# One mixer moved to the head of both transformer layers, and the attention steps moved off its products

## The chip, the cores and the metric

The kernel runs on one core of one Trainium2 chip. The metric is the device time of one execution in microseconds (us). The core has five engines that run beside each other: TensorE (PE, with its weight loads shown apart as PEld), VectorE (DVE), ScalarE (ACT), GpSimd (POOL) and SyncE (SP, which issues most DMAs). In the trace each engine's instructions stand in the order of its own list; where an operand isn't there yet the engine stands still, and what is behind in its list with it.

## The reference, cut to what matters

A first block (a Hyena layer, then grouped attention) is followed by a second block of two layers. The change lies in these two, so only they matter here. `x` has 256 tokens, and in the first of the two layers 256 context tokens go through the same work.

```
def trunk_layer(...):
    h = modulate(rmsnorm(x, g1), sh1, sc1)
    z = h @ w_in
    ...
    o = diff_attend(q, k, v, lam)                       # 4 heads, two score maps each
    mix = concat([mixer_a(z), mixer_b(z), mixer_c(z), diff_out(o)])
    x = x + gt1 * (mix @ w_out)
    x = x + gt2 * conv_ffn(...)

def mixer_a(z, ws, bs):
    u = gelu(group(z, G_AU))
    v = rmsnorm(gelu(group(z, G_AV)))                   # per head
    mixed = einsum('hpq,bcqhd->bcphd', ws, v) + bs
    return u * mixed
def mixer_b(z, w):  return group(z, G_BB) * dwconv3(group(z, G_BC) * group(z, G_BX), w)
def mixer_c(z):     return real(fft2(group(z, G_CF)))
```

The three mixers and the attention read only `z`; their shares of `mix @ w_out` are summed, so they may be computed in any order.

## The kernel before

Features lie on the partitions, tokens on the columns: n = 512 columns in layer 0 of the last block (256 latent and 256 context tokens) and n = 256 in layer 1. Every product is made in three passes over a high and a low half of each operand (`mm3`, lines L285 to L287: hi by hi, lo by hi, hi by lo). Weights come as 512 KB pieces (`wr`), which ACT casts to the high half `wh` (L281) and DVE subtracts for the low half `wl` (L282). A projection of a mixer (`proj_f`) is 24 such passes into one PSUM tile of the tag `mm`; there are four of these tiles, handed out in turn, so a tile comes back when its fourth predecessor has been read.

In each of the two layers this comes first: keys (`keys`, `heads_t(1)`), and then queries (`queries`, `heads_t(0)`), the latter two tokens blocks t = 0 and 1. `queries` turns q by a table on DVE (L1149 to L1156), splits and transposes it (`stack`, L1126, L1127, L1130, L1137), and also makes `gv` for mixer a out of the same PSUM tile: a gelu on ACT (L1167), a square and a sum on DVE (L1170, L1171, L374), a power on POOL (L378), and a scaling on DVE (L1174). In layer 0 the attention of the context tokens (`attend(range(4))`) is run to its end between keys and queries.

The attention of the latent tokens (`last4`) is a generator of 10 steps. A step holds for one q block the scores and two exponentials (`maps`, L1207 to L1214), for one two steps back its transposes (`turn`, L1224), and on every other one the product with v (`values`, L1233). After them stands the norm of the attention's result (`norm_d`, two parts). The steps are taken from a list `turns` of 13 entries, `[last4] * 10 + [nd, None, nd]`, one at each call of `turn_of`, and these calls stand behind the products of the mixers and, in `out_x`, behind every so many of the 8 output products (`every`). So a mixer or an output product is a carrier under whose PE work a step of attention runs.

`ORDER` sets which mixer comes first. In layer 0 the first mixer's output product follows it at once with a turn after each second product; in both layers the output product of mixer i comes behind mixer i + 1. Mixer a (`mixer_a`) multiplies `gv` by a table on PE (L1287, tile `pa`) between a gelu of its projection (L1282) and two DVE passes (L1290, L1292). Mixer c makes two small products one behind the other, with a split on ACT and DVE between.

The text of the kernel is not the order on the engines: a scheduler lists each engine's instructions by what it takes to be ready, and the loads of ACT's function tables (ACT_TABLE_LOAD, wherever the next function isn't in the table that is loaded) are put in behind it.

Of the kernel before, what the change touches and what calls it, by code (L numbers as in the profile page):

```python
# [32 lines left out]
STEPS = (2, 1, 2, 1)  # L33

LAG_G, LAG_D = (1, 3), (2, 2)
ORDER = ("bac", "cab")

N_ADA = 96
PACE = 0.6
# [193 lines left out]
def build(nc, tc, a, out, off, upto=99):  # L233
    with ExitStack() as es:
        _build(es, nc, tc, a, out, off, upto)


def _build(es, nc, tc, a, out, off, upto):
# [13 lines left out]
    def mmps(n=512):  # L252
        return pmm.tile([P, 512], F32, tag="mm", name="mm")[:, :n]
# [16 lines left out]
    def tmb(n=512):  # L270
        return rg.tile([P, 512], F32, tag="tb", bufs=4, name="tb")[:, :n]
# [4 lines left out]
    def pair(pool, shape, tag, bufs=1):  # L276
        return _Pair(pool.tile(shape, F32R, tag=tag + "h", name=tag + "h", bufs=bufs),
                     pool.tile(shape, F32R, tag=tag + "l", name=tag + "l", bufs=bufs))

    def split(dst, src):  # L280
        S.copy(dst.hi, src)  # L281
        V.tensor_tensor(dst.lo, src, dst.hi.bitcast(F32), op=ALU.subtract)  # L282
# [6 lines left out]
    def load_w(src, pool=None, step=True):  # L289

        raw = wp.tile([P, 1024], F32, tag="wr", bufs=NWR, name="wr")
        nc.sync.dma_start(raw, src.rearrange("p k c -> p (k c)"))
        if step:
            ada_step()
            av_step()
        w = pair(pool or wp, list(src.shape), "w", NW)
        split(w, raw.rearrange("p (k c) -> p k c", k=src.shape[1]))
        return w

    def load_c(src, i, step=True):  # L300

        return [load_w(src[2 * i + j], step=step) for j in range(2)]

    def proj_f(ps, w, h, cols, kt=8, m=0):
        for k in range(kt):
            mm3(ps, w[:, k, m * P:(m + 1) * P], h[:, k, cols], k == 0, k == kt - 1)
# [139 lines left out]
    def proj_o(ps, prods, m, c):  # L446

        for i, (ws, act) in enumerate(prods):
            for k in range(2):
                mm3(ps, ws[m // 4][:, k, (m % 4) * P:(m % 4 + 1) * P], act[:, k, c],  # L450
                    i + k == 0, i == len(prods) - 1 and k == 1)
# [3 lines left out]
    def turn_of():  # L455

        if turns:
            f = turns.pop(0)
            if f:
                next(f, None)  # L460

    def out_x(prods, n, gts, every=0):

        for m in range(8):
            ps = mmps(n)
            proj_o(ps, prods, m, slice(0, n))
            add_x(ps, m, n, gts)
            if every and m % every == every - 1:
                turn_of()
# [30 lines left out]
    def add_x(ps, m, n, gts):  # L500
        for j in range(n // 256):
            c = slice(256 * j, 256 * j + 256)
            V.scalar_tensor_tensor(xt[:, m, c], ps[:, c], gts[j][:, m:m + 1], xt[:, m, c],  # L503
                                   op0=ALU.mult, op1=ALU.add)
# [78 lines left out]
    def ada_upto(l, q):  # L583

        ada_step(max(0, 8 * (ada_q0[l] + q) - ada_done[0]))
        if ada_done[0] <= 8 * (ada_q0[l] + q) or ada_done[0] == N_ADA:
            ada_flush()
# [32 lines left out]
    def mod_part(l, v, part):  # L620
        return ada[l][:, v, 8 * part:8 * part + 8]
# [458 lines left out]
    for l in range(2):  # L1080
        ctx_out = l == 0
        n = 512 if ctx_out else 256
# [21 lines left out]
        gt1 = [mod_part(al, v, 2) for v in range(2)]  # L1104

        def mixer_w(j):

            if l == 0:
                ada_upto(al, 3)
            return [load_w(a["w_o"][l, c, j]) for c in range(2)]  # L1110
# [161 lines left out]
        def mixer_a(tag):  # L1272
            gws = tmb().rearrange("p (h s) -> p h s", h=4)
            nc.sync.dma_start(gws, a["gws"][l])
            w = load_c(a["w_f"][l], 0)
            mix = pair(a3, [P, 2, n], tag, 1 if tag == "at" else 512 // n)
            for m in range(2):
                ps = mmps(n)
                proj_f(ps, w[m], h, slice(0, n))
                turn_of()  # L1280
                gu = tmb(n)
                S.activation(gu, ps, AF.Gelu_apprx_tanh)  # L1282
                pa = mmps(n)
                for t in range(nt):
                    for hh in range(2):
                        hd = 2 * m + hh
                        T.matmul(pa[64 * hh:64 * hh + 64, t * P:t * P + P], gv[:, t, 64 * hd:64 * hd + 64], gws[:, hd, :],  # L1287
                                 start=True, stop=True, tile_position=(0, 64 * hh))
                ga = tmb(n)
                V.tensor_tensor(ga.rearrange("p (t q) -> p t q", q=P), pa.rearrange("p (t q) -> p t q", q=P),  # L1290
                                gbs[:, l, m, :].unsqueeze(1).to_broadcast([P, nt, P]), op=ALU.add)
                V.tensor_tensor(ga, ga, gu, op=ALU.mult)  # L1292
                split(mix[:, m, :n], ga)
            return mix
# [58 lines left out]
        held = None  # L1353
        for i, c in enumerate(ORDER[l]):
            mix = {"a": mixer_a, "b": mixer_b, "c": mixer_c}[c]("at" if i == 2 else "mix")
            if held:
                out_x([(mixer_w("abc".index(held[0])), held[1])], n, gt1, 4)
            held = c, mix
            if i == 0 and l == 0:
                out_x([(mixer_w("abc".index(c)), mix)], n, gt1, 2)  # L1360
                held = None
        while turns:
            turn_of()
        if l == 0:
            ada_upto(al, 5)
        ws = [[load_w(a["w_o"][l, c, j]) for j in ("abcd".index(ORDER[l][-1]), 3)] for c in range(2)]
        prods = [([ws[0][i], ws[1][i]], m) for i, m in enumerate((mix, mixd))]
# [89 lines left out]
```

## Time and profile before

| | |
|---|---|
| median of 3 runs | 1809.03 us (1806.14 to 1810.25) |
| the profiled execution | 1808.75 us, its span 1807.0 us |
| PE busy in the span | 1757.9 us (97%) |
| DVE busy, ACT busy | 1354.5 us (75%), 814.6 us (45%) |
| granted clock of TensorE, mean | 0.991 |
| layer 0's mixers and attention | 966 to 1060 us of the span |
| layer 1's mixers and attention | 1519 to 1600 us of the span |

PE's busy time is that of overlapping passes; a pass of 512 columns starts 0.23 us behind the last one when nothing is waited for, one of 256 columns 0.117 us. Where PE's next start is later than that, PE has stood still, and since it is busy nearly throughout, such time is what a change of order can add or remove.

### The profile page before, as it was taken

How to read it: one execution, taken by the hardware profiler on the slowest of the kernel's cores; microseconds unless marked ns; L12 is line 12 of the kernel's file. 1: busy time of each engine (PE TensorE's matmuls, PEld its weight loads, DVE VectorE, ACT ScalarE, POOL GpSimd, SP SyncE). 2: the span in 40 equal slices, each digit the busy share in tenths (PEclk: the TensorE clock that was granted, in tenths of full speed). 3: DMA queues.
4: the chain of work that ended last, by engine and by line, in shares of the span. 5: the costliest groups of instructions: out<-in, count | busy, mean ns of one | idle time of the engine just before them, and what ended most of it. 6: DMA issues, size and time to landing. Idle time of an engine off the chain costs nothing.

```text
span 1807.0 us, 27447 instructions
## 1 busy us (share of the span) xinstructions
PE 1757.9 (97%) x10602; PEld 1480.7 (82%) x10602; DVE 1354.5 (75%) x2449; ACT 814.6 (45%) x1447; POOL 43.0 (2%) x42
## 2 busy tenths in 40 slices
PE   6999999999999999999999999999999999999998
PEld 2778788787777888888878889788888887989997
DVE  6778577577666776888968867988667777878786
ACT  3433233334233354556578526332332337654444
POOL 0000000000000001000000000000000000000000
PEclk8999999999999999999999999999999999999999
DMA  8454434444444433333443223544544553346662
GB/s 333 173 175 161 147 130 139 152 147 137 140 155 146 151 111 118 118 113 119 144 141 115 76 68 101 180 147 154 157 151 145 194 175 112 106 129 199 187 186 83
DMA packets 73889, 262.62 MB, mean 145 GB/s; under 512 B 8288, under 2 KB 9632, under 8 KB 73120
## 3 DMA queue, kind: packets, MB, share of 16 engines
q1 hardware_dynamic: 71328, 254.71, 43.4%
q10 hardware_dynamic: 1856, 3.28, 0.6%
q0 software_dynamic: 576, 2.88, 0.5%
q8 instruction: 84, 1.38, 0.3%
q14 instruction: 45, 0.37, 0.1%
HBM read 259.79 MB, written 1.05 MB: 144 GB/s over the span
## 4 chain that ended last, share of the span: by engine, by line
PE 88%; DVE 6%; ACT 2%; issue 1%; DMA 1%; POOL 1%; SPq 0%; POOLq 0%; DVEq 0%; ACTq 0%
PE mm L285 25%; PE mm L286 24%; PE mm L287 24%; PE at L285 3%; PE at L287 2%; PE at L286 2%; PE ad L541 2%; DVE wl L282 1%; POOL rs_r L378 1%; PE tp L1011 1%; ACT wh L281 1%; PE tp L1130 1%; PE tp L1224 1%; PE at L388 1%; DVE t L412 1%
## 5 line engine op out<-in xcount | busy, mean ns | idle before, releaser
L281 ACT CAST wh<-wr 128x1024 fp32r<-128x1024 f32 x328 | 342.7, 1050 | 555.1 <-PE mm L286 493.4
L285 PE MATMUL mm<-hh,wh 128*128 128x512 f32 (+1 forms) x1568 | 550.0, 352 | 2.3 <-ACT hh L427 1.1
L286 PE MATMUL mm<-hl,wh 128*128 128x512 f32 (+1 forms) x1568 | 545.1, 348 | 1.1 <-DVE hl L844 1.1
L287 PE MATMUL mm<-hh,wl 128*128 128x512 f32 (+1 forms) x1568 | 544.0, 348 | 0.5 <-DVE wl L282 0.5
L282 DVE TENSOR_TENSOR wl<-wr,wh 128x1024 fp32r<-128x1024 f32 x328 | 399.2, 1219 | 189.0 <-ACT wh L281 188.3
L285 PEld LDWEIGHTS mm<-hh,wh 128*128 128x128 f32 x1568 | 295.0, 189 | 56.5 <-issue 11.9
L287 PEld LDWEIGHTS mm<-hh,wl 128*128 128x128 f32 x1568 | 295.0, 188 | 40.1 <-DVE wl L282 0.9
L286 PEld LDWEIGHTS mm<-hl,wh 128*128 128x128 f32 x1568 | 295.4, 189 | 38.5 <-DVE hl L844 1.7
L503 DVE SCALAR_TENSOR_TENSOR xt<-mm,ada,xt 128x256 f32<-128x256 f32 x352 | 153.6, 477 | 26.6 <-PE mm L287 25.2
L285 PE MATMUL mm<-fh,wh 128*128 128x256 f32 (+1 forms) x384 | 124.7, 326 | 0.4 <-DVE xt L503 0.4
L286 PE MATMUL mm<-fl,wh 128*128 128x256 f32 (+1 forms) x384 | 124.7, 326 | 0.0
L287 PE MATMUL mm<-fh,wl 128*128 128x256 f32 (+1 forms) x384 | 124.6, 325 | 0.0
L602 DVE CUSTOM_DVE_ANT_0 junk<-av,cb,vec 128x1024 f32<-128x1024 f32 x64 | 82.0, 1281 | 28.4 <-DMA av<-in_ada_dram 27.8
L285 PE MATMUL mm<-wh,hh 128*128 128x512 f32 x240 | 96.6, 405 | 3.1 <-DVE t L920 2.3
L286 PE MATMUL mm<-wl,hh 128*128 128x512 f32 x240 | 96.0, 400 | 0.7 <-DVE wl L282 0.7
L287 PE MATMUL mm<-wh,hl 128*128 128x512 f32 x240 | 96.1, 401 | 0.0
L378 POOL TENSOR_TENSOR rs_r<-rs_x,mhalf 128x4 f32<-128x4 f32 (+2 forms) x34 | 40.4, 1191 | 1719.7 <-DVE rs_x L374 1583.4
L285 PEld LDWEIGHTS mm<-fh,wh 128*128 128x128 f32 x384 | 72.7, 190 | 7.4 <-DVE xt L503 0.6
L286 PEld LDWEIGHTS mm<-fl,wh 128*128 128x128 f32 x384 | 72.9, 190 | 6.7
L287 PEld LDWEIGHTS mm<-fh,wl 128*128 128x128 f32 x384 | 72.8, 190 | 6.6
L541 PE MATMUL ad<-ar,sc_c 128*32 128x256 f32 x768 | 56.9, 407 | 5.7 <-DMA ar<-in_ada_dram 5.7
L286 PE MATMUL mm<-al,wh 128*128 128x512 f32 (+1 forms) x160 | 56.4, 354 | 0.0
(347 smaller groups left out, 2932.5 us busy)
## 6 DMA issues: line engine op xcount, KB each, us to landing
ar<-in_ada_dram SPq DMA_DIRECT2D x96, 512.0 KB, 4.4
wr<-in_w_u_dram SPq DMA_DIRECT2D x88, 512.0 KB, 3.7
wr<-in_hy_in_dram SPq DMA_DIRECT2D x64, 512.0 KB, 4.6
av<-in_ada_dram SPq DMA_DIRECT2D x48, 512.0 KB, 3.7
wr<-in_w_d_dram SPq DMA_DIRECT2D x44, 512.0 KB, 3.9
wr<-in_at_t_dram SPq DMA_DIRECT2D x24, 512.0 KB, 3.8
wr<-in_w_t_dram SPq DMA_DIRECT2D x24, 512.0 KB, 4.2
wr<-in_w_f_dram SPq DMA_DIRECT2D x20, 512.0 KB, 3.6
```

The lines of the kernel that those rows point to most:

```text
L281: S.copy(dst.hi, src)
L282: V.tensor_tensor(dst.lo, src, dst.hi.bitcast(F32), op=ALU.subtract)
L285: T.matmul(ps, l.hi, r.hi, start=first, stop=False)
L286: T.matmul(ps, l.hi, r.lo, start=False, stop=False)
L287: T.matmul(ps, l.lo, r.hi, start=False, stop=last)
L378: G.tensor_tensor(r, x, mhalf[:, :n], op=ALU.pow)
L388: T.matmul(ss[:, t * nb:(t + 1) * nb], sq[:, t * P:(t + 1) * P], col, start=(i == 0), stop=(i == len(sqs) - 1))
L412: V.tensor_tensor(sqs[0], sqs[0], q, op=ALU.add)
L503: V.scalar_tensor_tensor(xt[:, m, c], ps[:, c], gts[j][:, m:m + 1], xt[:, m, c], op0=ALU.mult, op1=ALU.add)
L541: T.matmul(ps[32 * j:32 * j + 32, :], sc_c[:, l // 2, k, :], raw[:, 256 * j:256 * j + 256], start=(k == 0), stop=(k == 7), tile_position=( ...
L602: V.tensor_tensor_reduce(junk, raw, cb[:, v, :], 1.0, vv("ab3")[:, i:i + 1], op0=ALU.mult, op1=ALU.add, accum_out=ada[3][:, v, i:i + 1])
L1011: T.transpose(tp[:, s * P:s * P + P], ps[hh, t][:, s * P:s * P + P], ident)
```

## The change

Mixer a becomes the first in both layers (`abc` in layer 0 for `bac`, `acb` in layer 1 for `cab`). The call of `turn_of` between a's two projections is gone, so no step stands under mixer a. The later output products take a turn after each second product in place of each fourth. In layer 0 the ten attention steps are now at a's output product (4) and at mixer b (6); in layer 1 at c (2), a's output product (4) and b (4 and the first part of the norm).

```diff
-ORDER = ("bac", "cab")
+ORDER = ("abc", "acb")
...
                 proj_f(ps, w[m], h, slice(0, n))
-                turn_of()
                 gu = tmb(n)
                 S.activation(gu, ps, AF.Gelu_apprx_tanh)
...
             if held:
-                out_x([(mixer_w("abc".index(held[0])), held[1])], n, gt1, 4)
+                out_x([(mixer_w("abc".index(held[0])), held[1])], n, gt1, 2)
```

**ACT in layer 0**, from the last steps of the context attention to the queries. `ath` is the split of the transposed map, `od` the copy of the attention's result, `gv` mixer a's second input, `tb` the output of a mixer's projection. Before:

```order
L1210 ACTIVATE t,sums<-at,dmx 128x256
L281 CAST ath<-tp 128x2x128
L1305 COPY tb<-mm 128x512
L1210 ACTIVATE t,dmx<-at,dmx 128x256
L281 CAST wh<-wr 128x1024
L1233 COPY od<-tp 64x256
L281 CAST ath<-tp 128x2x128
L1167 ACT_TABLE_LOAD
L1167 ACTIVATE gv<-mm 128x256
L281 CAST ath<-tp 128x2x128
```

Now:

```order
L1210 ACTIVATE t,sums<-at,dmx 128x256
L281 CAST ath<-tp 128x2x128
L1281 ACT_TABLE_LOAD
L1281 ACTIVATE tb<-mm 128x512
L1210 ACT_TABLE_LOAD
L1210 ACTIVATE t,dmx<-at,dmx 128x256
L1233 COPY od<-tp 64x256
L281 CAST ath<-tp 128x2x128
L1126 CAST t<-t 128x4x64 x2
L1167 ACT_TABLE_LOAD
L1167 ACTIVATE gv<-mm 128x256
L281 CAST ath<-tp 128x2x128
```

Mixer b's plain copy (L1305) has been replaced by mixer a's gelu with a table load on either side of it, ahead of the last exponential of the context attention; a third load follows with the gelu of `gv`. In the whole program there are 14 table loads for 13.

**PE at the same place**: `at<-ks,qs` are the last scores, `tp<-ath,vdh` and its like the product with v, `mm<-hh,wh` the passes of a mixer's projection.

```order
 L1207 MATMUL at<-ks,qs 128x256
-L285 MATMUL mm<-hh,wh 128x512
-L286 MATMUL mm<-hl,wh 128x512
-L287 MATMUL mm<-hh,wl 128x512
 L285 MATMUL tp<-ath,vdh 128x256
-L285 MATMUL mm<-hh,wh 128x512
-L286 MATMUL mm<-hl,wh 128x512
-L287 MATMUL mm<-hh,wl 128x512
 L286 MATMUL tp<-atl,vdh 128x256
 L287 MATMUL tp<-ath,vdl 128x256
```

Just behind it, now:

```order
L1224 MATMUL tp<-msk,t 128x128 x4
L285 MATMUL tp<-ath,vdh 128x256
L286 MATMUL tp<-atl,vdh 128x256
L287 MATMUL tp<-ath,vdl 128x256
L285 MATMUL tp<-ath,vdh 128x256
L286 MATMUL tp<-atl,vdh 128x256
L287 MATMUL tp<-ath,vdl 128x256
L1130 MATMUL tp<-msk,t 96x128 x8
L1286 MATMUL mm<-tb,gv 64x128 x2
L285 MATMUL mm<-hh,wh 128x512
```

The passes of a second projection stood between these products; now there are none until `gv` has been multiplied (L1286, which was L1287). The reason is the four `mm` tiles: before, the tiles behind the two of the queries go to b's first and second projection; now they go to a's first projection and to `pa`, so a's second projection needs the tile of the queries' block 0, which the gelu of `gv` reads.

**PE in layer 1**, at the transposes of the queries' block 0 (L1130). Before:

```order
L1130 MATMUL tp<-msk,t 96x128 x8
L286 MATMUL mm<-hl,wh 128x256
L287 MATMUL mm<-hh,wl 128x256
L285 MATMUL mm<-hh,wh 128x256
L1207 MATMUL at<-ks,qs 128x512 x2
L286 MATMUL mm<-hl,wh 128x256
```

Now:

```order
L1130 MATMUL tp<-msk,t 96x128 x8
L286 MATMUL mm<-hl,wh 128x256
L287 MATMUL mm<-hh,wl 128x256
L1207 MATMUL at<-ks,qs 128x512 x2
L1286 MATMUL mm<-tb,gv 64x128 x2
L285 MATMUL mm<-hh,wh 128x256
```

The product with `gv` block 0 now stands ahead of the second projection; the one with block 1 stands 24 passes and 8 transposes further on, and only behind that come mixer c's 48 passes and the second pair of scores.

## Rows read from the trace of the kernel before

**Rows 1.** The page: busy time by engine, and the chain that ended last.
```profile
PE 1757.9 (97%) x10602; PEld 1480.7 (82%) x10602; DVE 1354.5 (75%) x2449; ACT 814.6 (45%) x1447; POOL 43.0 (2%) x42
...
PE 88%; DVE 6%; ACT 2%; issue 1%; DMA 1%; POOL 1%; SPq 0%; POOLq 0%; DVEq 0%; ACTq 0%
```

**Rows 2.** Layer 0 by stretch: length, busy by engine, granted clock, DMA.
```profile
966.00:1010.00 44.00, 43.98 (x230) 35.95 (x229) 39.15 (x94) 30.61 (x72) 2.01 (x2) 1.00 0.25 79
1010.00:1027.00 17.00, 17.00 (x94) 14.21 (x93) 15.75 (x34) 9.59 (x22) 0.00 (x0) 1.00 0.18 60
...
1052.00:1060.00 8.00, 6.99 (x38) 5.68 (x36) 5.47 (x8) 3.38 (x6) 0.00 (x0) 1.00 0.22 66
```

**Rows 3.** Layer 1, one stretch, the same columns.
```profile
1526.00:1540.00 14.00, 10.30 (x55) 8.54 (x54) 11.27 (x26) 9.29 (x20) 1.82 (x1) 0.76 0.29 94
```

**Rows 4.** PE in order of time, layer 0: start, length, instruction, count.
```profile
973.42 0.28 PE L1207 MATMUL at<-ks,qs 96*128 96x256 f32 x1
...
975.64 0.38 PE L1224 MATMUL tp<-msk,t 128*128 128x128 f32 x2
...
976.55 0.38 PE L1224 MATMUL tp<-msk,t 128*128 128x128 f32 x2
...
979.64 1.26 PE L1130 MATMUL tp<-msk,t 128*96 128x128 f32 x8
```

**Rows 5.** ACT in order of time, the same place.
```profile
973.84 0.61 ACT L1305 COPY tb<-mm 128x512 f32<-128x512 f32 x1
974.32 0.51 ACT L1210 ACTIVATE t<-at,dmx 128x256 f32<-128x256 f32 x1
...
975.84 0.37 ACT L1233 COPY od<-tp 64x256 f32<-64x256 f32 x1
...
976.49 1.28 ACT L1167 ACT_TABLE_LOAD   x1
977.79 0.38 ACT L1167 ACTIVATE gv<-mm 128x256 f32<-128x256 f32 x1
...
978.32 0.72 ACT L1126 CAST t<-t 128x256 fp32r<-128x256 f32 x2
```

**Rows 6.** ACT's groups from 1027 to 1060 us: count, busy, mean ns.
```profile
L1282 ACT ACTIVATE tb<-mm 128x512 f32<-128x512 f32 x2 | 1.2, 594 | 0.0
```

**Rows 7.** DVE in order of time, layer 0, and what each waited for.
```profile
975.73 0.48 DVE L1214 SCALAR_TENSOR_TENSOR t<-t,dmx 128x256 f32<-128x256 f32 x1
...
979.01 0.42 DVE L1170 TENSOR_TENSOR t<-gv 128x256 f32<-128x256 f32 x1
...
981.57 0.43 DVE L1174 TENSOR_TENSOR gv<-gv,rs_r 128x256 f32<-128x256 f32 x1 [1.02 <-POOL rs_r L378]
...
982.12 0.68 DVE L1208 TENSOR_REDUCE dmx<-at 128x1 f32<-128x512 f32 x1
...
987.51 0.43 DVE L1174 TENSOR_TENSOR gv<-gv,rs_r 128x256 f32<-128x256 f32 x1 [1.19 <-POOL rs_r L378]
```

**Rows 8.** PE in order of time, layer 1, with idle time and releaser.
```profile
1523.52 0.73 PE L1207 MATMUL at<-ks,qs 96*128 96x512 f32 x2
...
1527.57 1.05 PE L1130 MATMUL tp<-msk,t 128*96 128x128 f32 x8 [0.96 <-DVE t L1127]
...
1531.17 0.49 PE L1207 MATMUL at<-ks,qs 96*128 96x512 f32 x1 [0.67 <-ACT t L1210]
1533.37 0.79 PE L1207 MATMUL at<-ks,qs 96*128 96x512 f32 x1 [1.70 <-ACT t L1210]
```

**Rows 9.** DVE in order of time, layer 1.
```profile
1525.84 0.42 DVE L1174 TENSOR_TENSOR gv<-gv,rs_r 128x256 f32<-128x256 f32 x1 [1.33 <-POOL rs_r L378]
...
1529.31 1.22 DVE L282 TENSOR_TENSOR wl<-wr,wh 128x1024 fp32r<-128x1024 f32 x1
1531.42 0.42 DVE L1174 TENSOR_TENSOR gv<-gv,rs_r 128x256 f32<-128x256 f32 x1 [0.90 <-POOL rs_r L378]
```

**Rows 10.** SP's DMA issues in order of time, merged.
```profile
1046.21 30.19 SPq L292 DMA_DIRECT2D wr<-in_w_u_dram  x4
```

## The prediction

> **What bounds the kernel now.** I read the page first: PE is busy 97% of the span, and the chain that ended last is 88% PE's [rows 1]. The number of passes is the same after the change, so the time moves by what PE stands still, no more and no less. I therefore looked for that in the two places that the change touches, stretch by stretch. In layer 0 there is nothing to win where the steps run: from 966 to 1027 us PE is busy 61.0 of 61 us, with DVE at 39.15 of 44 and 15.75 of 17 [rows 2]. The one loss, 1.0 us from 1052 to 1060, is at the end of mixer c, which stays last. In layer 1 there is something to win: from 1526 to 1540 us PE is busy 10.30 of 14 us and the granted clock is 0.76, so part of the stretch was at 1.2 GHz [rows 3]. There attention begins under mixer c while the queries are unfinished: PE waits for the queries' second block (1527.57), then twice for an exponential, 0.67 and 1.70 us [rows 8]. Then I put the new order of PE, ACT and DVE (from the lists) on the durations of these rows.
>
> **Layer 0: the end of the context attention.** Both orders are the same up to PE's last scores at 973.42 [rows 4]. On ACT a copy of 0.61 us stood next, and the last exponential began at 974.32 [rows 5]. Now a table load, a gelu and a table load stand there: 1.28 [rows 5] + 0.59 [rows 6] + 1.28, from about 973.95 to 977.1. From the exponential to the transposes that need it were 2.2 us (974.32 to 976.55) [rows 4, 5]; about 0.55 of that was rotary work of the queries on DVE, now already done, so I take 1.65: the transposes come at 978.75, 2.2 us later. This delay would cost nothing with PE work beside it; before, b's second projection (24 passes of 0.23 us) was that work. Now PE has, from 973.54, six passes with v (0.7) and one pair of transposes (0.3): it stands still for **4.2 us**.
>
> Next in ACT's list come the copy 0.37, the cast of the first transposes (as long), the casts 0.72, the load 1.28, the gelu of gv 0.38 and only then the cast of the last transposes [rows 5]: some 3.4 us from 977.8, so to 981.2. The product with v waits for it behind the transposes, done at 979.0: **2.6 us**, with 0.4 for the low half on DVE. Then the product (0.6), the queries' transposes (1.0) [rows 4] and 0.2 for a copy bring PE to 983.5.
>
> Now mixer a's product needs block 0 of gv. Before, gv's gelu began at 977.79 [rows 5] and the scaling ended at 982.0 [rows 7]: 4.2 us. The gelu now starts at 980.5; with a little less of other DVE work between, gv is there at about 984.4. PE waits **0.9 us**; before, nobody waited for gv, since a ran 50 us later. Then ten and two passes of a's second projection and the transposes of block 1, 3.6 us, to 988.2. Block 1 of gv comes through gelu, square, power and scaling once more, ending at 989.5 by the same count (before, 987.94 [rows 7]): **1.3 us**. At the output product of a the split of a's second half is late by **0.35 us**. Sum 4.2 + 2.6 + 0.2 + 0.9 + 1.3 + 0.35 = 9.55, less 0.2 that PE lost at the transposes before: **+9.4 us**. TensorE will very likely be granted its lower clock behind this spell; most of that is hidden, since the waits for gv hang on ACT, DVE and POOL and would only get shorter.
>
> Bounds: at the least the first delay stays, 2.8 us of exponential with no cover (PE idle 2.8), and the gelu's load behind it; I take 5 as the low end. The high end adds a backlog on DVE: a's output product now carries four score pairs and two turns where b's carried two and four. A score pair is two reductions of 0.68 [rows 7] and about 1.1 of small work (estimated from the 0.48 of half the width [rows 7]), a turn about 0.7: 3.5 us more than the 15.75 of 17 [rows 2]. The split of b's second weight is queued behind it; b's first projection (5.6 us) covers it by about 1 us by my count, and without that cover PE would wait up to 3. So 5 to 13.
>
> **Layer 1.** From the queries' transposes at 1522.2 to the point at 1557.4 where both orders have done the same work, PE's passes take about 27 of the 35.2 us: 8.3 lost, waits and low clock together. In the new order the losses are others. After the scores (done at 1524.0 [rows 8]) PE needs gv block 0, there at 1526.26 [rows 9]: 2.3 us, and 0.3 at either side. Eight passes, the transposes of block 1 at 1527.6, sixteen passes, to 1530.3; then gv block 1. It was there at 1531.84, but a weight split of 1.22 us [rows 9] now stands ahead of the sum's scaling on DVE where a split of 0.41 stood, so 1532.6: 2.3 us. Then mixer c's 48 passes run without a wait, and they aren't a cover for attention any more: the second and third score pairs stand behind them, with the exponentials between, a table load ahead of them, and c's small products waiting for splits in the same ACT list. I count 1.1 + 0.7 + 0.6 + 0.3 + 0.2 = 2.9 there, and 0.6 at a's dense output product. Together 8.4 against 8.3: nothing gained at full clock. These waits are longer than those of [rows 8], in whose stretch the clock fell: a mean of 0.76 over 14 us is 6.7 us at 1.2 GHz [rows 3]. A spell half as long behind the second wait would fall on c's 48 passes and lose 1.7 us. I take **+1 us**, with -5 (only the waits for gv remain, less what DVE does faster) and +4 as ends.
>
> **What costs nothing.** The table for mixer a is now loaded earlier; for layer 1 it stands between loads of `w_u`. Those four issues were spread over 30 us from 1046 [rows 10], so SP has room for its wait on c's passes; without that room each weight would come later by as much. The second part of the attention's norm moves into the last output product, with 36 of its 48 passes still to run.
>
> **Sum.** 1808.75 (the profiled execution, 0.3 below the median of the runs) + 9.4 + 1.0 = **1819.2 us**.
>
> **Rivals.** (1) *Faster.* Layer 1 wins all 8.3 us since a's products fill what c left open, and layer 0 loses only the low end, 5: 1805.5. For it speaks that the wait on an exponential [rows 8] does go; against it that PE's list has the gv products ahead of the passes that would fill. It decides once layer 1 wins more than layer 0 loses. (2) *Unchanged*: layer 0 at 5 and layer 1 at -4, 1809.8. That the change doesn't do what it says is part of it: a score pair still stands inside mixer a in layer 1, and ACT has 14 table loads for 13. (3) *DVE becomes the bound* at a's output product in layer 0: 3 us on top, 1822.2. For it, 93% of DVE's time in the stretch before [rows 2]; against it, PE had no wait there. (4) *A table change costs more than its load.* Between load and gelu are 0.02 us [rows 5]: 976.49 + 1.28 to 977.79. If each of the three loads ahead of PE's waits cost twice 1.28, the time were 1819.2 + 3.8 = 1823.
>
> The Trainium skill, "ScalarE: Activation LUTs", section "What ACT_TABLE_LOAD costs", has for a change of table a load of 1283 ns and a drain of about 1380 ns, 2.66 us in all. By that page the sum would be 1819.2 + 3 x 1.38 = 1823.3, an estimate; the rows show the load alone, and no drain. Its "Rules for kernel authors" ask that functions of one table be done together before the next; the order on ACT now alternates gelu and exp more than before.
>
> **Numbers.** Forecast (1819.2, own range 1813 to 1824) 0.65; (3) 0.15; (4) 0.04; unchanged 0.10; faster 0.06. The range from 1811 to 1826 takes in the bounds 5 and 13 with layer 1 near its middle, and leaves out the faster case and half of the unchanged one. What can be told from no change is 0.2%, 3.6 us: faster 0.06, same 0.10, slower 0.84.
>
> **What would show it.** In layer 0, PE idle 7 us or more between the last context scores and the first product with gv, with two table loads between the exponentials; a first wait for the transposes' operand (DVE) near 3 us, then one for the cast on ACT near 2; no wait in b's projections. In layer 1, two waits of about 2.3 us for gv in place of those for exponentials, and a granted clock below 1 in both places. Wrong if PE's list shows no wait at the product with v in layer 0, or if layer 1's stretch up to b gets shorter by more than 4 us.

## The result, and the profile after

| | before | after |
|---|---|---|
| median of the runs beside each other | 1808.76 us (4 runs, 1806.14 to 1810.25) | 1821.33 us (4 runs, 1818.57 to 1824.35) |
| ratio, 95% interval | | 1.0067 [1.0052, 1.0082] |
| the profiled execution, its span | 1808.75, 1807.0 us | 1818.57, 1816.8 us |
| granted clock, mean | 0.991 | 0.993 |

The kernel is slower by 0.67%, 12 us. The profiled execution is the fastest of the four; the three others had a mean granted clock of 0.986 to 0.990. It is 9.8 us behind that of before, and all of this arises in layer 0: from PE's last context scores (973.42 [rows 4], now 973.37) to the first scores of layer 1 (1523.52 [rows 8], now 1533.51) the stretch has grown from 550.10 to 560.14 us, by 10.0; behind that point nothing more is lost.

The page's busy line and its chain of work that ended last, to be read against [rows 1]:

```profile
PE 1761.8 (97%) x10602; PEld 1480.2 (81%) x10602; DVE 1355.6 (75%) x2449; ACT 816.2 (45%) x1448; POOL 42.3 (2%) x42
...
PE 87%; DVE 5%; ACT 3%; DMA 2%; issue 1%; POOL 1%; SPq 0%; POOLq 0%; DVEq 0%; ACTq 0%
```

They say nearly nothing: ten microseconds are half a per cent of the span, and PE stays at 97%. The view by stretches says where to look. Layer 0, the columns of [rows 2], with the stretch of low clock and that of a's output product as its last lines:

```profile
966.00:1010.00 44.00, 38.89 (x203) 29.73 (x202) 33.60 (x86) 27.60 (x60) 2.01 (x2) 0.92 0.16 48
1010.00:1027.00 17.00, 17.00 (x85) 13.98 (x84) 14.70 (x28) 9.44 (x22) 0.00 (x0) 1.00 0.33 101
...
978.90:985.60 6.70, 5.30 (x21) 3.86 (x22) 4.43 (x14) 4.80 (x9) 1.01 (x1) 0.50 0.00 0
...
994.00:1008.00 14.00, 13.99 (x62) 10.60 (x61) 13.59 (x29) 7.04 (x14) 0.00 (x0) 1.00 0.12 38
```

In the first 44 us PE was busy 43.98, now 38.89, and for 6.7 us TensorE had 1.2 GHz. In the next 17 us PE loses nothing. (DVE's 14.70 there and the 15.75 of [rows 2] belong to different work, since the order has moved.) PE in order of time in the first stretch, the engine of [rows 4]; in brackets its idle time and who ended it:

```profile
973.37 0.28 PE L1207 MATMUL at<-ks,qs 96*128 96x256 f32 x1
973.95 0.38 PE L285 MATMUL tp<-ath,vdh 128*128 128x256 f32 x1 [0.31 <-ACT ath L281]
974.89 0.39 PE L286 MATMUL tp<-atl,vdh 128*128 128x256 f32 x1 [0.55 <-DVE atl L282]
...
978.81 0.62 PE L1224 MATMUL tp<-msk,t 128*128 128x128 f32 x2 [2.84 <-ACT t L1126]
980.83 0.58 PE L285 MATMUL tp<-ath,vdh 128*128 128x256 f32 x1 [1.40 <-ACT ath L281]
981.36 0.58 PE L286 MATMUL tp<-atl,vdh 128*128 128x256 f32 x1
...
982.60 1.91 PE L1130 MATMUL tp<-msk,t 128*96 128x128 f32 x8
984.44 0.70 PE L1286 MATMUL mm<-tb,gv 128*64 128x128 f32 x4
...
989.20 0.88 PE L1286 MATMUL mm<-tb,gv 128*64 128x128 f32 x12
...
994.02 0.50 PE L285 MATMUL mm<-mixh,wh 128*128 128x512 f32 x1
```

ACT beside it, which [rows 5] showed for before:

```profile
973.92 1.28 ACT L1281 ACT_TABLE_LOAD   x1
975.21 0.60 ACT L1281 ACTIVATE tb<-mm 128x512 f32<-128x512 f32 x1
975.83 1.28 ACT L1210 ACT_TABLE_LOAD   x1
977.13 0.47 ACT L1210 ACTIVATE t<-at,dmx 128x256 f32<-128x256 f32 x1
...
978.84 1.28 ACT L1167 ACT_TABLE_LOAD   x1
980.13 0.38 ACT L1167 ACTIVATE gv<-mm 128x256 f32<-128x256 f32 x1
980.41 0.37 ACT L281 CAST ath<-tp 128x256 fp32r<-128x256 f32 x1
```

The last exponential has moved from 974.32 [rows 5] to 977.13 behind load, gelu and load; PE stands at the transposes of its result. The bracket of that wait names ACT's cast of the queries (L1126), which ended beside it; what the transposes read is DVE's row L1214, made from the exponential:

```profile
978.18 0.48 DVE L1214 SCALAR_TENSOR_TENSOR t<-t,dmx 128x256 f32<-128x256 f32 x1
```

The next load stands ahead of the cast for which the product with v waits. The two scalings of `gv` on DVE, as in [rows 7]:

```profile
983.25 0.43 DVE L1174 TENSOR_TENSOR gv<-gv,rs_r 128x256 f32<-128x256 f32 x1 [1.02 <-POOL rs_r L378]
...
988.19 0.43 DVE L1174 TENSOR_TENSOR gv<-gv,rs_r 128x256 f32<-128x256 f32 x1 [1.18 <-POOL rs_r L378]
```

Both are done just ahead of PE's products with `gv` (984.44 and 989.20), which therefore show no wait. In layer 1, PE in order of time, beside [rows 8]:

```profile
1536.32 0.44 PE L1286 MATMUL mm<-tb,gv 128*64 128x128 f32 x4 [2.07 <-DVE gv L1174]
...
1541.89 0.66 PE L1286 MATMUL mm<-tb,gv 128*64 128x128 f32 x8 [0.57 <-DVE gv L1174]
...
1551.62 0.50 PE L1207 MATMUL at<-ks,qs 96*128 96x512 f32 x1 [1.76 <-ACT t L1210]
```

Two waits for `gv` and one for an exponential stand there for the waits of before; the spell at 1.2 GHz behind them, as a stretch, is half of the 6.7 us that [rows 3] came to:

```profile
1552.30:1555.70 3.40, 3.40 (x14) 3.17 (x15) 2.90 (x7) 1.72 (x4) 0.00 (x0) 0.50 0.52 153
```

### The profile page after: what moved, and what is told of

Same layout as the page of the kernel before. It is cut to its first block, busy times and chain, and to the rows that moved or that the text cites. A ratio compares the mean times of both kernels' runs of the same rounds, so it can differ in the third digit from the quotient of the medians.

```text
span 1816.8 us, 27437 instructions
## 1 busy us (share of the span) xinstructions
PE 1761.8 (97%) x10602; PEld 1480.2 (81%) x10602; DVE 1355.6 (75%) x2449; ACT 816.2 (45%) x1448; POOL 42.3 (2%) x42
## 4 chain that ended last, share of the span: by engine, by line
PE 87%; DVE 5%; ACT 3%; DMA 2%; issue 1%; POOL 1%; SPq 0%; POOLq 0%; DVEq 0%; ACTq 0%
PE mm L285 24%; PE mm L286 24%; PE mm L287 24%; PE at L285 3%; PE ad L541 3%; PE at L287 2%; PE at L286 2%; DVE wl L282 1%; POOL rs_r L378 1%; DMA ar<-in_ada_dram 1%; PE tp L1011 1%; ACT wh L281 1%; PE at L388 1%; PE at L1207 0%; PE at L401 0%
```

## The experiments

In all of them the ratio is against the kernel before, run on the same chip. Beside it stands, in the table at the end, a number from the traces, the **layer 0 stretch**: from PE's last context scores to the first scores of layer 1, all the same work; before 550.10, after 560.14 us. Each is the difference of two rows of PE's order of time, in one execution. The ratio is taken over all runs and needn't equal the quotient of two medians. The expectations give the two first waits of the change as 3.06 and 1.76 us, counted by what lies between two starts beyond a pass's usual distance; the brackets, counted from the end of what ran before, have 2.84 and 1.40.

### The two layers apart

Layer 0 of the change alone, and layer 1 of the change alone; in the other layer the step in mixer a and the spacing of the steps are those of before too:

```diff
-ORDER = ("abc", "acb")
+ORDER = ("abc", "cab")
```
```diff
-ORDER = ("abc", "acb")
+ORDER = ("bac", "acb")
```

> Layer 0 as in the changed kernel (a first, no step between its products), layer 1 as before. Theory: the whole loss lies at layer 0's start, where PE stands still 3.06 us ahead of the last transposes and 1.76 us ahead of the product with v, and then runs 6.8 us at 1.2 GHz; layer 1 gives and takes the same. Then this kernel is 8 to 12 us above the kernel before (ratio 1.0045 to 1.0065), with the same two waits. Rival: layer 1 carries a good part of the loss (its waits for gv, 2.24 and 0.84 us, and 1.98 us in mixer c); then this one is only 0 to 6 us above.

> Layer 0 as before, layer 1 as in the changed kernel (a, c, b). Theory: the waits for exponentials (0.67 and 1.70 us) and their low-clock spell of 6.8 us are exchanged for waits for gv (about 2.2 and 0.8 us) and one in mixer c (about 2 us) with a shorter spell: -2 to +2 us against the kernel before (ratio 0.999 to 1.001). Rival: layer 1 loses by itself, +3 us or more; other rival: it wins, -4 us or more, and layer 0 loses more than 10 us.

Layer 0 alone: 1820.14 us, ratio 1.0061 [1.0046, 1.0077]; layer 1 alone: 1810.43 us, 1.0004 [0.9993, 1.0016]. The theory held in both: the loss is layer 0's, and layer 1 exchanges one set of waits for another. PE's order of time in the first has the same two waits, and in the second the same waits for `gv` as the whole change:

```profile
979.65 0.66 PE L1224 MATMUL tp<-msk,t 128*128 128x128 f32 x2 [2.84 <-ACT t L1126]
981.68 0.58 PE L285 MATMUL tp<-ath,vdh 128*128 128x256 f32 x1 [1.36 <-ACT ath L281]
```
```profile
1525.88 0.44 PE L1288 MATMUL mm<-tb,gv 128*64 128x128 f32 x4 [2.08 <-DVE gv L1174]
1531.45 0.66 PE L1288 MATMUL mm<-tb,gv 128*64 128x128 f32 x8 [0.57 <-DVE gv L1174]
```

### The remaining parts of the diff

The spacing of the steps alone, on the kernel before, and the change with mixer a's step kept:

```diff
-                out_x([(mixer_w("abc".index(held[0])), held[1])], n, gt1, 4)
+                out_x([(mixer_w("abc".index(held[0])), held[1])], n, gt1, 2)
```
```diff
                 proj_f(ps, w[m], h, slice(0, n))
+                turn_of()
```

> The kernel before with one part of the change alone: the later output products take a step after each second product in place of each fourth; orders and mixer a's step as before. In layer 0 the ten steps are used up before this counts; in layer 1 the steps are drawn forward. Theory: this part is worth nothing, ratio 0.999 to 1.001. Rival: it is a loss or a gain of its own of 2 us or more that in the change was set off by the order of layer 1.

> The changed kernel with the step between mixer a's products kept, so that only the orders and the spacing of the later steps are changed. Theory: the loss is that of the order (a ahead of its inputs), not of the missing steps: within 3 us of the changed kernel (1818 to 1824), the waits of 3.06 and 1.76 us in layer 0 as in the changed one, since the first step comes behind them. Rival: the steps under a were what covered it: 4 us or more below the changed kernel; other rival: exponentials between two gelus add two table loads each and it is 3 us or more above.

The spacing: 1810.16 us, 1.0006 [0.9997, 1.0015], nothing that can be told. The step kept: 1823.68 us, 1.0080 [1.0066, 1.0094], with the same first waits (2.86 and 1.36). It is not faster than the change, perhaps slower: the intervals overlap, but its layer 0 stretch is 3.3 us longer, with a longer spell at 1.2 GHz, and ACT has 16 table loads for 14, as its second rival named. So the order carries the loss, and the missing step does not add to it.

### Table loads, and cover for PE

Three kernels change mixer a in layer 0 only: an exponential for the gelu (no table change around it; the gelu is left out), another PSUM pool for the product with the table (so that the second projection isn't held by the queries' tile), and both.

```diff
-                S.activation(gu, ps, AF.Gelu_apprx_tanh)
+                S.activation(gu, ps, AF.Exp if l == 0 else AF.Gelu_apprx_tanh)
```
```diff
-                pa = mmps(n)
+                pa = atps(n) if l == 0 else mmps(n)
```

> The changed kernel with the gelu of mixer a's own projection in layer 0 replaced by an exponential (the gelu is left out), so that ACT needs no change of table around it; PE's order up to the queries' first transposes is the same. Theory: the table loads are the first wait. Without the two loads of 1.28 us the wait ahead of the last transposes falls from 3.06 to about 0.5 us, the one ahead of the product with v stays at 1.5 to 2 (its load, that of gv's gelu, is still there), and the kernel is 2.5 to 5 us below the changed one. Rival: the missing passes on PE alone are the cause and the loads ran beside other delays: the first wait stays above 2 us and the time within 1 us of the changed kernel. Rival of a table change that costs twice its load: the wait is gone and the kernel is 5 to 8 us below.

> The changed kernel with mixer a's product with its table in layer 0 put into a PSUM tile of the other pool (that of the scores) in place of the mm pool. Its second projection then gets an mm tile that nobody holds, and its 24 passes stand on PE between the last products of the context attention. Theory: the tile held by the queries' gelu took PE's cover away; with it back, the waits of 3.06 and 1.76 us go (under 0.5 each) and the kernel is 6 to 10 us below the changed one, near the kernel before. Rival: the chain on ACT is the bound whatever PE has; the waits come again a few us later, at the products with gv, and the time is within 3 us of the changed kernel. Second rival: the tile taken from the scores delays the attention of the latent tokens and costs 2 to 4 us of the gain.

> The two edits of layer 0 together: exponential for gelu in mixer a's own projection (the gelu left out, so two table loads fewer ahead of the last exponential) and the product with the table in the scores' PSUM pool (so a's second projection stands on PE meanwhile). Theory (corrected): the chain on ACT and DVE from the last context exponential through the queries to gv sets when mixer a can end; a's 24 passes only decide at which link PE waits for it. Then each edit alone is worth what it takes off that chain: the loads 4 to 5 us, the tile 0 to 2, both together about the loads alone: 1815 to 1818. Rival (the first theory, cover on PE): with cover and a shorter chain the waits meet their cover, and the two are worth more together than the sum of both: 1811 to 1814.

Without the loads: 1816.69 us, 1.0039 [1.0025, 1.0053], 4.6 us below the change by the medians; the layer 0 stretch of the profiles has 3.0 of it (560.14 less 557.17). PE at the same two places:

```profile
977.52 0.41 PE L1224 MATMUL tp<-msk,t 128*128 128x128 f32 x2 [0.33 <-DVE t L1214]
979.66 0.39 PE L285 MATMUL tp<-ath,vdh 128*128 128x256 f32 x1 [1.72 <-ACT ath L281]
```

The first wait falls by 2.51 us, from 2.84 to 0.33: two loads of 1.28 and nothing else. The second stays (1.72 for 1.40), since the load of `gv`'s gelu does.

With the other PSUM pool: 1819.33 us, 1.0056 [1.0042, 1.0071]. This went against my theory (6 to 10 us won): it is 2 us by the medians, and the intervals overlap. The 24 passes did move in between, and both waits went; PE in order of time then shows new ones, and most of them lie in a spell at 1.2 GHz:

```profile
982.47 0.39 PE L285 MATMUL tp<-ath,vdh 128*128 128x256 f32 x1 [0.43 <-ACT ath L281]
...
985.37 0.70 PE L1286 MATMUL at<-tb,gv 128*64 128x128 f32 x4 [1.07 <-DVE gv L1174]
...
988.48 1.91 PE L1130 MATMUL tp<-msk,t 128*96 128x128 f32 x8 [0.77 <-DVE t L1127]
991.29 2.83 PE L1286 MATMUL at<-tb,gv 128*64 128x128 f32 x24 [0.90 <-DVE gv L1174]
...
996.16 2.08 PE L285 MATMUL mm<-mixh,wh 128*128 128x512 f32 x4 [0.46 <-ACT mixh L281]
```

That spell in the view by stretches:

```profile
985.40:999.00 13.60, 11.40 (x53) 7.93 (x54) 9.56 (x18) 6.71 (x13) 1.01 (x1) 0.50 0.22 77
```

From the last context scores (975.00) to the first pass of a's output product (996.16) are 21.2 us; in the change these are 20.65 (973.37 to 994.02). The passes were taken from one place and were missing at the next: what is behind `gv` came no earlier. The spell at 1.2 GHz is twice as long as that of the change, so part of the 21.2 us is the clock's and not the chain's; the trace doesn't part them. With both edits: 1816.31 us, 1.0041 [1.0026, 1.0057], as much as the loads alone, with a wait of 2.27 us for the second block of `gv` and two of 0.45 and 0.69. So what the corrected theory forecast came, and what the first one did, that these 24 passes are the cover that is missing, did not.

### The link to gv taken out

If the chain through `gv` is what counts, a mixer a that doesn't need the latent blocks of `gv` must lose little, table loads and all. In the change, and in the kernel with the other PSUM pool, the product now takes the context tokens' blocks twice, and that with the latent blocks is left out:

```diff
-                        T.matmul(pa[64 * hh:64 * hh + 64, t * P:t * P + P], gv[:, t, 64 * hd:64 * hd + 64], gws[:, hd, :],
+                        T.matmul(pa[64 * hh:64 * hh + 64, t * P:t * P + P], gv[:, t if l else 2 + t % 2, 64 * hd:64 * hd + 64], gws[:, hd, :],
```

> The changed kernel, but in layer 0 mixer a's product with its table reads the blocks of gv of the context tokens in place of those of the latent tokens too (the product with the latent blocks is left out). Those blocks are there before the context attention ends. Table loads, mm tiles and ACT's order up to gv's gelu stay. The product needs nothing of the queries, so that its tile can be read and handed on; but the second projection still waits for the tile of the queries' block 0 (its gelu). Theory (the chain to gv is the bound, not the passes): with the last link, gv, out of a's way, the passes of a's second half and of its output product stand ahead of the rest of the chain; the waits of 3.06 and 1.76 us shrink or go and the kernel is 4 to 9 us below the changed one (1812 to 1817). Rival (the end of the context attention alone is the chain: exponential, transposes, cast, product with v): the waits stay as they are and the time is within 2 us of the changed kernel.

> The same edit (latent blocks of gv left out of layer 0's product) together with the product's tile in the scores' PSUM pool. Nothing of mixer a waits for the queries then. Theory: PE has a's two projections, both products and the output product of a, some 140 passes, to lay beside the chain, as it had b's in the kernel before: the kernel comes within 3 us of the kernel before (ratio 0.999 to 1.002), the three table loads still there. Rival: the table loads cost their 4 to 5 us whatever stands on PE: 1813 to 1815 (ratio 1.002 to 1.0035).

1812.30 us, 1.0024 [1.0015, 1.0034], and 1813.68 us, 1.0022 [1.0010, 1.0035]. About 8 of the 12 us are gone. The first time lies in the range of its theory (1812 to 1817); the second lies outside that of its theory, by a little, and inside that of its rival (1813 to 1815). ACT's list at the place is that of the change, load by load (in order of time, the first kernel):

```profile
976.63 1.28 ACT L1210 ACT_TABLE_LOAD   x1
977.93 0.47 ACT L1210 ACTIVATE t<-at,dmx 128x256 f32<-128x256 f32 x1
...
979.65 1.28 ACT L1167 ACT_TABLE_LOAD   x1
```

Yet PE was busy 43.47 and 43.99 of the 44 us from 966 (38.89 in the change), at full clock, with no wait over 0.33: behind the context attention stood a's second projection, its products and its output product. The two kernels in the view by stretches:

```profile
966.00:1010.00 44.00, 43.47 (x245) 35.05 (x244) 38.50 (x99) 31.69 (x69) 2.01 (x2) 1.00 0.18 52
```
```profile
966.00:1010.00 44.00, 43.99 (x240) 35.00 (x239) 38.60 (x102) 32.30 (x75) 2.01 (x2) 1.00 0.16 49
```

The chain itself has not become shorter. From PE's last context scores to the end of the second scaling of `gv` it took 14.5 us before ([rows 4, 7]), 15.2 in the change, 16.2 with the other pool, and with early `gv` 16.6 in the first kernel (from 974.16) and 16.7 in the second. The row of the first:

```profile
990.29 0.42 DVE L1174 TENSOR_TENSOR gv<-gv,rs_r 128x256 f32<-128x256 f32 x1 [0.59 <-POOL rs_r L378]
```

So what differs is whether PE needs its end. The early products also give their PSUM tile back at once, so this edit frees the second projection too; that alone was worth about 2 us by the medians (above). The traces don't support the rival of the second, that the loads cost 4 to 5 us whatever stands on PE, since PE waits nowhere for them: the layer 0 stretch there is 1.9 us above before. What remains of 0.2% I can't place. Part of it in the first kernel's profile is a spell far from the change (granted clock 0.50 from 1475.5 to 1478.8); in the second's, 3.4 us stand there already at the last context scores (976.86 for 973.42), ahead of anything that was changed.

### Other mixers first

Mixer c first in layer 0; and mixer b first in layer 1 (b, a, c as shown, and b, c, a), with a step at each second output product there and layer 0 as before:

```diff
-ORDER = ("bac", "cab")
+ORDER = ("cab", "cab")
```
```diff
-ORDER = ("bac", "cab")
+ORDER = ("bac", "bac")
```

> The kernel before with mixer c first in layer 0 (c, a, b); layer 1 and the steps as before. c has 48 independent passes like a, but no gelu and no gv. Theory (what matters is that nothing of the first mixer hangs on queries or on a change of table): no wait of 3 us ahead of the last transposes, and 0 to 5 us above the kernel before (its small products wait for their own splits, 1.3 us each): ratio 1.000 to 1.003. Rival (the number of independent passes, 48 against b's 72, is what counts): 6 to 10 us above, ratio 1.003 to 1.0055.

> Layer 0 as before; in layer 1 mixer b first (b, a, c), its step kept, a step at each second output product. Theory: what hides the start of an attention is the number of PE passes that need nothing of queries or attention. In layer 1 mixer b has 72 of them (8.4 us at 0.117), c has 48 and c's small products wait by themselves, a has 48 of which half stand behind gv. The kernel before lost 8.3 us at layer 1's start with c first; with b first 3 to 7 us come back: ratio 0.996 to 0.998, and the granted clock stays at 1 there. Rival: the exponentials bound the start whatever runs beside them (the order of mixers in layer 1 is worth nothing, as a first was): 0.9995 to 1.001. Rival: c at the end of layer 1 brings its own wait (1.3 us in layer 0) with nothing behind it: 1.000 to 1.002.

> Layer 0 as before; in layer 1 b, c, a, with a step at each second output product. Theory as for b, a, c: 3 to 7 us below the kernel before (ratio 0.996 to 0.998), and if c's own wait at the end is what limits b, a, c, this one is 1 to 2 us below that. Rival: no change, 0.9995 to 1.001.

Mixer c first: 1815.49 us, 1.0037 [1.0024, 1.0050]. No wait of 3 us at the transposes, as the theory said, but a loss of 6 us, outside its range (0 to 5) and in that of the rival (6 to 10), by which the number of independent passes counts. It lies a little later, where the latent attention begins:

```profile
988.33 0.50 PE L1207 MATMUL at<-ks,qs 96*128 96x512 f32 x1 [1.88 <-ACT qs L1137]
989.50 0.49 PE L1207 MATMUL at<-ks,qs 96*128 96x512 f32 x1 [0.66 <-ACT t L1210]
991.11 0.62 PE L1207 MATMUL at<-ks,qs 96*128 96x512 f32 x1 [1.12 <-ACT t L1210]
```

So a first mixer without `gv` and without a change of table loses too: the link to `gv` is not the only way to lose here. That its 48 passes against b's 72 are the reason fits the time, but no run shows it by itself.

Mixer b first in layer 1: 1808.67 us, 0.9999 [0.9990, 1.0008], and 1809.24 us, 0.9998 [0.9987, 1.0010]. My theory of 3 to 7 us back fell. The start is better, as it said: in b, a, c the clock stays at 1.00 and PE is busy 12.05 of 14 us for 10.30 [rows 3]. What follows gives it back. The stretches of that kernel from 1526, and PE's wait in mixer c from its order of time:

```profile
1526.00:1540.00 14.00, 12.05 (x94) 11.21 (x93) 12.72 (x30) 11.75 (x24) 1.01 (x1) 1.00 0.23 77
1540.00:1560.00 20.00, 20.00 (x161) 18.21 (x160) 19.72 (x39) 15.39 (x33) 0.00 (x0) 1.00 0.34 113
1560.00:1580.00 20.00, 17.70 (x145) 16.83 (x145) 17.89 (x38) 11.68 (x23) 3.06 (x2) 1.00 0.42 139
```
```profile
1578.78 0.39 PE L285 MATMUL mm<-t_cn,t 128*128 128x256 f32 x1 [1.37 <-ACT t L281]
```

From 1560 to 1580 PE is busy 17.70 us, where the kernel before has 19.99 of 20:

```profile
1560.00:1580.00 20.00, 19.99 (x166) 19.40 (x165) 17.96 (x35) 13.15 (x29) 0.00 (x0) 1.00 0.49 152
```

DVE works 19.72 of 20 us ahead of that, and PE's first wait behind it is for DVE:

```profile
1561.47 0.38 PE L286 MATMUL tp<-atl,vdh 128*128 128x256 f32 x1 [0.71 <-DVE atl L282]
```

In b, c, a the same wait is 1.28 us, at 1561.42, and c's own wait is not there. So the rows show c's wait and one for DVE; that DVE is the next limit is not shown beyond that. No kernel of the study beats the one before.

| kernel | ratio | layer 0 stretch, us over before | last context scores to a's output product, us |
|---|---|---|---|
| the change | 1.0067 | 10.0 | 20.65 |
| layer 0 alone | 1.0061 | 10.5 | 21.15 |
| step kept | 1.0080 | 13.3 | 24.31 |
| other PSUM pool | 1.0056 | 10.3 | 21.16 |
| no table change | 1.0039 | 7.1 | 18.99 |
| both | 1.0041 | 6.4 | 18.35 |
| early gv | 1.0024 | 3.3 | 11.18 |
| early gv, other pool | 1.0022 | 1.9 | 12.12 |
| c first | 1.0037 | 5.8 | |

The last column is the chain up to the end of mixer a (with a pair of scores in it where a step stands there; with early `gv`, one block of the queries lies behind it). Whether PE's 24 passes stand early or late in it, it keeps its length within 0.7 us, and the loss goes with it.

## Why the prediction was right, and where not

**The time.** 1819.2 us was forecast; the median is 1821.33, in the range, and slower. The profiled execution, against which the sum was made, is 1818.57.

**Layer 0, the sum.** +9.4 was forecast; the traces have +10.0, and layer 0 alone 1.0061, 11 us. Step by step: the last transposes were put at 978.75 and came at 978.81; the low half for the product with v was put at about 981.6 and came at 981.36; the first product with `gv` at 984.4 and came at 984.44; the second block of `gv` at 989.5 and was there at 988.62.

**Terms that were mis-sized.** The wait at the last transposes was put at 4.2 and is 3.70 with the two short ones ahead of it (0.31, 0.55, 2.84); that at the product with v was put at 2.6 and is 1.40. So the idle time up to the first product with `gv` is 5.1 us, and the sign named for it, 7 us or more, was not seen. The waits for `gv` (0.9 and 1.3) did not show, nor the 0.35 at a's output product. The low clock, which I had put down as mostly hidden, took their place: eight transposes of the queries take 1.91 us for 1.26 [rows 4], and PE came to the product with `gv` 0.8 us after `gv` was there (983.68). The stretch at 1.2 GHz holds 5.30 us of PE's busy time; half of that, 2.65 us, is an estimate of what it cost. With the 5.1 that makes some 7.8 of the 10.0; the last 2 us I did not trace. One kind of loss stood for the other, and that the sum came out so near is luck in part.

**The reason given for it, the step that failed.** I wrote that the delay "would cost nothing with PE work beside it", took 24 passes for that work, and had named, ahead of the prediction, the `mm` tile that the queries hold as what takes them away. That work on PE hides the delay was right: with early `gv` the loss is mostly gone. That these 24 passes were enough was wrong. With the tile free and the passes back, about 2 us were won by the medians, and the waits came again at `gv`. The delay is that of a chain, by the order of ACT's list: last exponential, transposes, product with v, queries, gelu, square, power and scaling of `gv`, for both blocks. (The gelu itself reads only the queries' projection, L1167; it stands behind the rest in the list.) The chain is about as long in the kernel before, where nothing waits for its end. Mixer a has just 48 passes (11.2 us at 0.23) which don't hang on it, and these are needed once, wherever they stand; its output product, the next cover, is behind `gv`. Mixer b in its place needs nothing of the chain and has its output product behind it as well. The runs without the link to `gv` show it; they give PE more independent passes and take the link away in one, so the two are not parted. The two table loads lengthen the chain's way to the first block of `gv` by 1.7 us (10.3 for 8.6, to the end of the first scaling) and were worth some 4 to 5 us by the medians, 3.0 in the profiles' layer 0 stretch.

**Layer 1.** +1 was forecast; the traces have -0.2 (9.8 less 10.0) and the run of its own +0.7 [-1.3, +2.9]. The first wait for `gv` (2.3 forecast) is 2.07, that for the exponential behind mixer c's passes 1.76 (2.9 for all that was counted there); the second for `gv` is 0.57 for 2.3 (counted from the first scores, the block came 0.8 us sooner and PE 1.0 us later than was put down), and the 0.6 at a's output product is not seen.

**The rivals.** *Faster* and *unchanged* are out. *DVE becomes the bound*: at a's output product DVE was busy 13.59 of 14 us, so what spoke for this rival was there, but PE was busy 13.99 of 14 and waited for nothing; out. *A table change costs more than its load*: in every row shown the function begins 0.01 to 0.02 us behind the load's end (973.92 + 1.28, then 975.21), and taking two loads away took 2.51 us from the wait. The Trainium skill, "ScalarE: Activation LUTs", section "What ACT_TABLE_LOAD costs", has a drain of about 1380 ns beside the load; by it the two loads would take 5.3 us, an estimate. The measurement decides: no drain here. **What costs nothing**: the spacing of the steps, which moves the later turns of the norm too, measured 1.0006 [0.9997, 1.0015]; the earlier load of mixer a's table was not run by itself, and layer 1 alone, which has it, measured 1.0004.

## What to carry to other kernels

Ask of the piece of work that is put first behind a serial chain how much of it, and of what follows it in the list, needs nothing of that chain's end; cover that is only moved forward is missing later. Work that needs the chain's last link belongs last, whatever tiles it holds; and to be without that link isn't enough, as mixer c showed, which needs no `gv` and still lost 6 us when it came first. A change of function table on the engine that carries the chain cost its load in full where PE stood waiting for it, and no wait for it was seen where PE had other work. And a start that was made faster gave nothing here, since new waits came behind it.

## What the runs showed of the hardware that I had not expected

The granted clock differs between executions at a place where the instruction lists are the same. From 941.7 us on, ahead of anything that was changed, the profiled executions of before (first) and after had:

```profile
941.70:945.10 3.40, 3.40 (x13) 3.02 (x13) 2.46 (x7) 2.72 (x7) 1.05 (x1) 0.50 0.54 170
```
```profile
941.70:945.10 3.40, 3.40 (x19) 2.65 (x18) 2.46 (x7) 3.40 (x8) 1.05 (x1) 1.00 0.61 173
```

Nor is the length of a spell the kernel's alone: at the same two waits of layer 0 it was 6.7 us in the change and 10.1 in the kernel with layer 0 alone (0.50 from 977.4 to 987.5). So a difference of 2 us between two profiles is not yet one between kernels. That there is a spell at such waits is common to them, and with early `gv` there is none at this place.
